# ScalarE and VectorE in program order, and seven products for gate and up in a feed-forward trunk

## The chip, the cores and the metric

The kernel runs on one core of a Trainium2 chip. The metric is the device time of one execution in microseconds (us). A core has TensorE (PE; its weight loads are listed as PEld), VectorE (DVE), ScalarE (ACT), GpSimd (POOL) and SyncE (SP), each with its own queue, and 16 DMA engines that they share.

## The reference

Two layers. Each layer adds half of a gated feed-forward to x, then two attentions of one input projection, then half of a second feed-forward. So there are four feed-forward stages, of this form:

```python
def rms_norm(x, g):
    y = x * rsqrt(mean(x * x, -1) + 1e-6)
    return y * g
def swiglu(h, w_gate, w_up, w_down):
    return (silu(h @ w_gate) * (h @ w_up)) @ w_down
x = x + 0.5 * swiglu(rms_norm(x, ffn_norm[l]), w_gate[l], w_up[l], w_down[l])
```

x is 256 tokens by 1024 features, the hidden width is 2816, everything is float32. A last RMSNorm gives the output.

## The kernel before

**Operands in two parts.** Every float32 operand of a large matmul is split into a high part, rounded to the float32r format, and the rest, also float32r. A product is then three matmuls: high by high, low by high, high by low (`tokens`, L323 to L332). The split of a weight tile is made in `emit_load` (L91 to L119): SP loads the raw tile (L100), ScalarE casts it to the high part (L116), VectorE subtracts (L117), in two halves of 128 x 1024 elements. Raw, high and low tiles have three buffers each (N_RAW, N_HI, N_LO). `specs` lists the weight tiles in the order of use; `weights()` (L122 to L129) gives the next one and has loads and splits written up to LOOK = 2 tiles ahead.

**A feed-forward stage** (`ffn`, L397) goes through the hidden width in groups of 512 columns: group 0, then groups 1 to 4 in a loop, then a last piece of 256 gate and 256 up columns. For a group, gate and up (256 tokens by 512 columns each) are 4 weight tiles of 512 features by 512 columns; each tile is 24 matmuls of 128x128 by 128x512 (4 chunks of features, 2 halves of the tokens, 3 matmuls). `hidden` takes them out of PSUM: ScalarE's SiLU (L402), VectorE's product (L408). `turn` transposes the hidden tile on TensorE (8 transposes, L70), and ScalarE and VectorE split it (L336, L337). `down` adds the group's part of the down product to four PSUM banks that stay for the whole stage (2 tiles, 48 matmuls). So a loop turn is 96 + 48 matmuls and 8 transposes. The other four PSUM banks go round.

**The norm** (`Norm`, L174) isn't applied ahead of the matmuls: x is transposed in four pairs of 128-feature blocks (`pair`), scaled by the gain and split (`operands`, L197 and L198); the row factor, from the sums of squares (L183) and a power on POOL (L208), is applied to the outputs. The residual sums (L382) of the second half and the last two pairs come inside the next stage's first group (`late`).

**What sets the order.** Matmuls and transposes outside a few attention parts are kept in program order (`mm`, `flip`). The instructions of the other engines are ordered by a scheduler at build time, from priorities and an estimated timeline; `urgent` raises the priority of what takes results out of PSUM. Each engine then runs its queue strictly in order.

Of the kernel before, what the change touches and what calls it, by code (L numbers as in the profile page):

```python
# [27 lines left out]
LOOK = 2  # L28
N_RAW, N_HI, N_LO = 3, 3, 3
N_S4 = 18  # L30
# [3 lines left out]
def trunk(ctx: ExitStack, tc: tile.TileContext, x, n1, g1, u1, d1, nm, w_in, sink,  # L34
          lq1, lk1, lq2, lk2, subln, w_out, n2, g2, u2, d2, nf, out):
    nc = tc.nc
    pe, act, dve, pool, sp = nc.tensor, nc.scalar, nc.vector, nc.gpsimd, nc.sync
# [27 lines left out]
    def mm(*a, **k):  # L65

        tc.keep_in_program_order(pe.matmul(*a, **k))  # L67

    def flip(*a):
        tc.keep_in_program_order(pe.transpose(*a))  # L70

# [4 lines left out]

    specs = []
    loaded = {}
# [7 lines left out]
    def plain(w, c0, n, k0=0, kn=None):  # L86
        src = rows(w, c0, n, k0, kn)
        kn = src.shape[1]
        return (kn, n, lambda t: [(t, src)])

    def emit_load(i):  # L91
        kn, n, moves = specs[i]
        raw = wp.tile([P, kn, n], F32, tag="raw", bufs=N_RAW, name=nm_("raw"))
# [4 lines left out]
        for dst, src in moves(raw):  # L98
            if i > 1:
                sp.dma_start(dst, src)  # L100
            else:
                for a, b in zip(cuts, cuts[1:]):
                    sp.dma_start(dst[:, a:b], src[:, a:b])  # L103
                    yield
# [15 lines left out]
    nxt = [0, 0]  # L120

    def weights():  # L122
        i = nxt[0]
        nxt[0] += 1
        while i > 1 and nxt[1] <= min(i + LOOK, len(specs) - 1):
            for _ in emit_load(nxt[1]):
                pass
            nxt[1] += 1
        return loaded.pop(i)  # L129

    for l in range(DEPTH):
        def ffn_specs(wg, wu, wd):
# [3 lines left out]
            for g in range(1, NGRP):  # L136
                specs.extend(plain(w[l], g * 512, 512, k0, 4) for w in (wg, wu) for k0 in (0, 4))
                specs.extend(down(g - 1, h) for h in range(2))
            for k0 in (0, 4):
                def gu_moves(t, k0=k0, ws=(wg[l], wu[l])):  # L140
                    return [(t[:, :, h * 256:h * 256 + 256], rows(w, FF - 256, 256, k0, 4)) for h, w in enumerate(ws)]
                specs.append((4, 512, gu_moves))
# [10 lines left out]
        for c in range(2):  # L153
            def qa_moves(t, c=c, wi=wi):
                return [(t[:, :, h * P:(h + 1) * P], rows(wi, QA + h * 256 + c * P, P)) for h in range(2)]
            paired.add(len(specs))
            specs.append((KC, 256, qa_moves))
# [5 lines left out]
        for k0 in (0, 2):  # L163
# [3 lines left out]
            specs.append((2, D, o_moves))  # L167
# [6 lines left out]
    class Norm:  # L174


        def __init__(self, g0):
            self.g0, self.xs = g0, []
            self.ss = tmp("nss", 2, (P, 2, 4))

        def squares(self, t, c, n):
            j_ = tmp("junk", 2, (P, 512))
            act.activation(j_[:, :n], xk[:, t, c:c + n], AF.Square, accum_out=self.ss[:, t, c // 256:c // 256 + 1])  # L183

        def pair(self, j):
            sl = halves(bank())
            for i in range(2):
                for t in range(2):
                    flip(sl[:, i, t * P:(t + 1) * P], xk[:, t, (2 * j + i) * P:(2 * j + i + 1) * P], ident)
            with urgent():  # L190
                self.operands(j, sl)

        def operands(self, j, sl):
            xs = blk()
            for i in range(2):
                g = gcol[:, self.g0 + 2 * j + i:self.g0 + 2 * j + i + 1]
                self.last_act = act.activation(xs[:, i, 0:S], sl[:, i], AF.Identity, scale=g)  # L197
                self.last = dve.scalar_tensor_tensor(xs[:, i, S:512], in0=sl[:, i], scalar=g, in1=f(xs[:, i, 0:S]),  # L198
                                                     op0=ALU.mult, op1=ALU.subtract)
            self.xs.append(xs)  # L200
# [11 lines left out]
        def spread(self, sl):  # L212
# [4 lines left out]
            mm(sl[:, 0:S], lhsT=ones, rhs=dg, start=True, stop=True)  # L217
# [7 lines left out]
    pool.dma_start(grow1, n1.rearrange("l (k p) -> (l k) p", p=P))  # L225
    early = [emit_load(0), emit_load(1)]
# [4 lines left out]
    nxt[1] = 2  # L231
# [13 lines left out]
    def take_x(k):  # L245

        if k < 4:
            norm.pair(k)
            for e in early * 2 if k < 2 else ():
                next(e)  # L250
        else:
            with tc.issue_after(norm.last_act.ins):
                for t in range(2):
                    for h in range(2):
                        norm.squares(t, h * 512, 512)
            norm.stats()

    grow = const.tile([NG - 16, P], F32, name="grow")
    dist_i = const.tile([P, 512], mybir.dt.int32, name="dist_i")
# [7 lines left out]
    lin = const.tile([P, 4, DEPTH * 64], F32, name="lin")  # L267
    lsum = const.tile([P, 2, DEPTH], F32, name="lsum")
    lpr = const.tile([P, 2, DEPTH * 64], F32, name="lpr")
# [5 lines left out]

    def attention_constants():
        for i, g in enumerate((nm, n2)):
            pool.dma_start(grow[i * 16:(i + 1) * 16], g.rearrange("l (k p) -> (l k) p", p=P))
        pool.dma_start(grow[32:34], subln)
# [3 lines left out]

        pool.iota(dist_i, pattern=[[P, 2], [-1, S]], base=0, channel_multiplier=1)
        dflat = distB.rearrange("p a b -> p (a b)")
        aflat = distA.rearrange("p a b -> p (a b)")
        dve.tensor_copy(aflat, dist_i)
# [3 lines left out]


        for c in range(4):
            pool.memset(qscA[0:64, c:c + 1], -0.125 / slopeA[c])
            pool.memset(qscA[64:128, c:c + 1], -0.125 / slopeA[c + 4])
            pool.memset(qscB[:, c:c + 1], -0.125 / slopeB[c])


        pool.dma_start(snk_in, sink.rearrange("l h -> (l h)").partition_broadcast(P))
        sv = snk_in.rearrange("p (l s c) -> p l c s", l=DEPTH, s=2)  # L300
        for t in range(2):
            for l in range(DEPTH):
                pool.tensor_copy(snk[:, l, :, t, :], sv[:, l])
        pool.tensor_scalar(nsnk.rearrange("p a b c d -> p (a b c d)"), snk.rearrange("p a b c d -> p (a b c d)"),
                           -1.0, 0.0, op0=ALU.mult, op1=ALU.add)

        for i, a in enumerate((lq1, lk1, lq2, lk2)):
            pool.dma_start(lin[:, i], a.rearrange("l d -> (l d)").partition_broadcast(P))

    def make_lam():  # L310
        for i in range(2):
            pool.tensor_tensor(lpr[:, i], lin[:, 2 * i], lin[:, 2 * i + 1], op=ALU.mult)
# [10 lines left out]
    def tokens(accs, xs, w, k0, ks=range(4), first=0, last=KC - 1, order=None):  # L323

        hi, lo = w
        for k, t in (order or [(k, t) for k in ks for t in range(2)]):
# [3 lines left out]
            mm(accs[t], lhsT=xh, rhs=hi[:, k], start=kk == first, stop=False)  # L330
            mm(accs[t], lhsT=xl, rhs=hi[:, k], start=False, stop=False)
            mm(accs[t], lhsT=xh, rhs=lo[:, k], start=False, stop=kk == (last if isinstance(last, int) else last[t]))  # L332
# [11 lines left out]
    def narrow(acc, w, j, xs, kcs, first, last):  # L344

        hi, lo = w
        for i, (wk, xk) in enumerate(kcs):
# [3 lines left out]
            mm(acc, lhsT=wh, rhs=xv[:, 0:S], start=first and i == 0 and j == 0, stop=False)  # L351
            mm(acc, lhsT=wh, rhs=xv[:, S:512], start=False, stop=False)
            mm(acc, lhsT=wl, rhs=xv[:, 0:S], start=False, stop=last and i == len(kcs) - 1 and j == 1)

    def first_groups(norm, ws):

        sls = [halves(bank()) for _ in ws]
        for k in range(0, KC, 2):
            if k:
                norm.late(k // 2 + 1)  # L360
# [12 lines left out]
    class Residual:  # L373
# [5 lines left out]
        def add(self, h, t):  # L379
            xv = xk[:, t, h * 512:(h + 1) * 512]  # L380
            with urgent():
                dve.tensor_tensor(xv, xv, self.accs[h][t], op=ALU.add)  # L382

        def turn(self, h):
            for j in (2 * h, 2 * h + 1):
                self.nxt.pair(j)
# [3 lines left out]
        def late(self, k):  # L390

            if k == 2:
                self.turn(1)
            elif k == 3:
# [431 lines left out]
```

## Time and profile before

| | |
|---|---|
| median of 3 runs | 979.01 us (977.41 to 979.86) |
| the profiled execution | 977.06 us, its span 975.3 us |
| granted TensorE clock, mean | 0.998 |
| ScalarE busy | 475.1 us (49%) |
| read from HBM | 167.54 MB, 173 GB/s over the span |
| a raw tile of 1024 KB, issue to landing | median 4.9 to 5.1 us |

The profile is one execution. A line of a group gives the source line, the engine, the operation, output and inputs with shapes and how often; behind the first bar the busy time and the mean of one in ns; behind the second the idle time of the engine just ahead, and what ended it. A line of the timeline gives start, duration and instruction. The chain of work follows what ended last back to the start. Busy PE is modelled: matmuls overlap, so the time from one start to the next counts, not the duration of one.

### The profile page before, as it was taken

The numbers are of one execution on the slowest core, as the hardware profiler recorded it, in microseconds if no ns is written. First come the engines' busy times: TensorE is split into PE (matmuls) and PEld (weight loads), VectorE is DVE, ScalarE is ACT, GpSimd is POOL, SyncE is SP. The second block draws the span as 40 slices with busy tenths as digits, with TensorE's granted clock in tenths as the row PEclk, the third lists the DMA queues.
The fourth block names the chain that finished last, engine by engine and source line by source line (L and its number), as shares of the span: only waits on it lengthen the run. The fifth ranks groups of instructions, "written<-read, shape, count | busy, mean of one in ns | idle before, by whom it ended". The sixth has DMA issues, their size and how long they took to land.

```text
span 975.3 us, 12345 instructions
## 1 busy us (share of the span) xinstructions
PE 954.0 (98%) x4940; PEld 808.2 (83%) x4940; DVE 555.4 (57%) x850; ACT 475.1 (49%) x779; POOL 22.0 (2%) x50
## 2 busy tenths in 40 slices
PE   7999999999999999999999999999999999999997
PEld 5788888899897888888888888888999878888886
DVE  4755455569955554454565454456797455554453
ACT  5643443458834543434464443436576454434433
POOL 4000000000000000000000000000000000000001
PEclk9999999999999999999999999999999999999999
DMA  9655565545523655555555555555553246565531
GB/s 275 228 199 173 180 208 173 185 149 179 137 87 130 215 173 183 200 179 194 193 174 175 191 196 176 200 184 173 174 148 112 87 173 197 191 202 202 179 130 43
DMA packets 98217, 169.38 MB, mean 174 GB/s; under 512 B 3182, under 2 KB 30896, under 8 KB 98160
## 3 DMA queue, kind: packets, MB, share of 16 engines
q1 hardware_dynamic: 96784, 167.26, 52.4%
q0 software_dynamic: 288, 0.30, 0.4%
q10 hardware_dynamic: 1088, 1.05, 0.3%
q8 instruction: 38, 0.62, 0.3%
q14 instruction: 19, 0.16, 0.0%
HBM read 167.54 MB, written 1.05 MB: 173 GB/s over the span
## 4 chain that ended last, share of the span: by engine, by line
PE 93%; DVE 3%; DMA 2%; issue 1%; ACT 0%; SPq 0%; POOLq 0%; POOL 0%
PE ps L67 85%; PE ps L70 3%; DMA raw<-in_ffn_w_gate_dram 2%; DVE wlo L117 2%; PE ps L547 1%; PE ps L612 1%; PE ps L633 1%; PE ps L635 1%; PE ps L634 1%; PE ps L652 1%; DVE s L198 1%; DVE xk L382 0%; ACT whi L116 0%; ACT s L197 0%; SPq L103 0%
## 5 line engine op out<-in xcount | busy, mean ns | idle before, releaser
L67 PE MATMUL ps<-whi,s 128*128 128x512 f32 (+1 forms) x2252 | 697.9, 391 | 7.4 <-DVE s L198 5.6
L117 DVE TENSOR_TENSOR wlo<-raw,whi 128x1024 fp32r<-128x1024 f32 (+2 forms) x392 | 379.5, 1014 | 322.6 <-ACT whi L116 320.5
L67 PEld LDWEIGHTS ps<-whi,s 128*128 128x128 f32 x2252 | 420.1, 188 | 96.4 <-DVE s L198 8.2
L116 ACT CAST whi<-raw 128x1024 fp32r<-128x1024 f32 (+2 forms) x392 | 323.8, 882 | 344.0 <-PE ps L67 299.1
L67 PE MATMUL ps<-wlo,s 128*128 128x512 f32 (+1 forms) x1126 | 437.8, 389 | 0.0
L67 PEld LDWEIGHTS ps<-wlo,s 128*128 128x128 f32 x1126 | 211.7, 188 | 43.5
L67 PE MATMUL ps<-s,whi 128*128 128x256 f32 x448 | 82.7, 286 | 0.4 <-DVE s L198 0.4
L67 PEld LDWEIGHTS ps<-s,whi 128*128 128x128 f32 x448 | 70.1, 192 | 1.6 <-DVE s L198 0.8
L67 PE MATMUL ps<-s,wlo 128*128 128x256 f32 x224 | 63.3, 283 | 0.0
L402 ACT ACTIVATE tmp<-ps,r 128x512 f32<-128x512 f32 (+1 forms) x48 | 31.2, 651 | 61.7 <-PE ps L67 61.7
L408 DVE SCALAR_TENSOR_TENSOR s<-ps,hr,tmp 128x512 f32<-128x512 f32 (+1 forms) x48 | 32.7, 705 | 36.9 <-PE ps L67 27.4
L67 PEld LDWEIGHTS ps<-s,wlo 128*128 128x128 f32 x224 | 42.9, 192 | 0.0
L557 ACT ACTIVATE s<-s,negm 128x256 f32<-128x256 f32 x64 | 31.8, 498 | 9.6 <-DVE negm L555 9.6
L337 DVE TENSOR_TENSOR s<-ps,s 128x512 fp32r<-128x512 f32 x48 | 31.0, 683 | 6.1 <-ACT s L336 6.1
L197 ACT ACTIVATE s<-ps,gcol 128x256 fp32r<-128x256 f32 x48 | 21.7, 472 | 21.9 <-PE ps L70 19.0
L336 ACT CAST s<-ps 128x512 fp32r<-128x512 f32 x48 | 25.8, 583 | 9.5 <-PE ps L70 9.5
L198 DVE SCALAR_TENSOR_TENSOR s<-ps,gcol,s 128x256 fp32r<-128x256 f32 x48 | 22.2, 480 | 11.0 <-ACT s L197 10.6
L70 PE MATMUL ps<-ident,s 128*128 128x128 f32 x208 | 27.3, 272 | 0.0
L70 PEld LDWEIGHTS ps<-ident,s 128*128 128x128 f32 x208 | 24.3, 141 | 3.3
L183 ACT ACTIVATE junk<-xk 128x512 f32<-128x512 f32 x24 | 15.0, 627 | 14.2 <-DVE xk L382 14.2
L208 POOL TENSOR_TENSOR r<-ms,mhalf 128x2 f32<-128x2 f32 x6 | 4.2, 705 | 628.1 <-DVE ms L206 628.1
L382 DVE TENSOR_TENSOR xk<-xk,ps 128x512 f32<-128x512 f32 x20 | 13.6, 681 | 3.8 <-PE ps L67 3.8
(109 smaller groups left out, 347.4 us busy)
## 6 DMA issues: line engine op xcount, KB each, us to landing
raw<-in_ffn_w_down_dram SPq DMA_DIRECT2D x44, 1024.0 KB, 4.9
raw<-in_ffn_w_gate_dram SPq DMA_DIRECT2D x39, 1024.0 KB, 5.0
raw<-in_ffn_w_up_dram SPq DMA_DIRECT2D x39, 1024.0 KB, 5.0
raw<-in_w_in_dram SPq DMA_DIRECT2D x14, 1024.0 KB, 5.1
raw<-in_ffn_w_gate_dram SPq DMA_DIRECT2D x8, 512.0 KB, 3.6
raw<-in_ffn_w_up_dram SPq DMA_DIRECT2D x8, 512.0 KB, 4.6
raw<-in_w_in_dram SPq DMA_DIRECT2D x8, 512.0 KB, 4.4
raw<-in_w_out_dram SPq DMA_DIRECT2D x4, 1024.0 KB, 4.7
```

Of the source, the lines that this page charges most:

```text
L67: tc.keep_in_program_order(pe.matmul(*a, **k))
L70: tc.keep_in_program_order(pe.transpose(*a))
L116: act.copy(h_, r_)
L117: dve.tensor_tensor(l_, r_, f(h_), op=ALU.subtract)
L183: act.activation(j_[:, :n], xk[:, t, c:c + n], AF.Square, accum_out=self.ss[:, t, c // 256:c // 256 + 1])
L197: self.last_act = act.activation(xs[:, i, 0:S], sl[:, i], AF.Identity, scale=g)
L198: self.last = dve.scalar_tensor_tensor(xs[:, i, S:512], in0=sl[:, i], scalar=g, in1=f(xs[:, i, 0:S]), op0=ALU.mult, op1=ALU.subtract)
L336: act.copy(dst[:, :, 0:S], src)
L337: dve.tensor_tensor(dst[:, :, S:512], src, f(dst[:, :, 0:S]), op=ALU.subtract)
L402: act.activation(g[:, :n], acc, AF.Silu, scale=norm.r[:, t:t + 1])
L408: dve.scalar_tensor_tensor(h[:, t, :n], in0=acc, scalar=norm.hr[:, t:t + 1], in1=g, op0=ALU.mult, op1=ALU.mult)
L557: act.activation(e[:, t, c], e[:, t, c], AF.Exp, scale=-1.0, bias=negm[:, n:n + 1], accum_out=den[:, n:n + 1])
```

## The change

**Program order.** ScalarE and VectorE, as TensorE, are wrapped so that each instruction outside attention is kept in program order. `urgent` and the other hints go.

**Seven products.** In groups 1, 3 and 4 of each stage (`SEVEN`), gate and up together are seen as a product of 2 by 2 blocks: token halves by feature halves, and feature halves by (gate, up). Strassen's scheme in Winograd's form does it in seven block products of 12 matmuls, in place of eight. `make_sums` forms the four sums of activation blocks once for each stage, each split into two parts; for them, `operands` keeps unsplit copies (`xg`), made on ScalarE. The sums of weight blocks are made in the raw tiles: with A, D the upper and lower gate blocks and B, C the upper and lower up blocks, step 0 uses A; step 1 B + C, where the C is added to the loaded B by a DMA from POOL's queue; step 2 A + B + C, by VectorE in the same tile; step 3 is a tile of the down matrix; step 4 D; step 5 A + B + C + D, by VectorE; step 6 A + B, where the B is added to the tile of A by a DMA, after step 2's sum; step 7 C; step 8 the second down tile. Each sum is split into high and low as any tile. `by_seven` runs the products in the order p1, p7, p6, down, p2, p4, p5, p3, down, and VectorE adds them up.

**Loads.** Raw tiles have six buffers, and loads run up to eight steps ahead of use (`AHEAD`); splits stay two ahead. Blocks of activations have 16 buffers in place of 18. POOL's constants are written at the start; what makes lambda moves from behind the first feed-forward into `attention_constants`, which is called ahead of group 3 of the first stage.

**Smaller moves.** SiLU is written right behind the gate's matmuls. In `ffn_close` and at the end of attention the next norm's first pairs are transposed earlier and among the last matmuls, and the residual sums of the first half after attention are made in quarters.

```diff
-LOOK = 2
-N_RAW, N_HI, N_LO = 3, 3, 3
-N_S4 = 18
+LOOK, AHEAD = 2, 8
+N_RAW, N_HI, N_LO = 6, 3, 3
+N_S4 = 16
+SEVEN = (1, 3, 4)
...
+            def call(*a, **k):
+                ins = issue(*a, **k)
+                if kept[0]:
+                    tc.keep_in_program_order(ins)
+                return ins
...
+    pe, act, dve = Kept(nc.tensor), Kept(nc.scalar), Kept(nc.vector)
...
+        def gather(k, to):
+            def add():
+                pool.dma_start(raws[to], w[k], accum_op=ALU.add)
+            return add
+        def plus(x, to):
+            def prep():
+                for h in (0, 2):
+                    x_, t_ = [raws[i][:, h:h + 2] for i in (x, to)]
+                    dve.tensor_tensor(t_, t_, x_, op=ALU.add)
+            return prep
...
+        return [Step(4, 512, load(a), key=a, free=[]),
+                Step(4, 512, load(b), key=b, behind=gather(c, b), free=[]),
+                Step(**n, prep=both(plus(a, b), gather(b, a)), src=b, free=[]),
+                downs[0],
+                Step(4, 512, load(d), key=d, free=[]),
+                Step(**n, prep=plus(b, d), src=d, free=[b, d]),
+                Step(**n, src=a),
+                Step(4, 512, load(c), key=c),
+                downs[1]]
...
+    def ahead(n):
+        n = min(n, len(specs) - 1)
+        while True:
+            if at["split"] <= n and at["prep"] > at["split"]:
+                for _ in emit_split(at["split"]):
+                    pass
+                at["split"] += 1
+            elif at["prep"] <= min(n + 1, len(specs) - 1) and at["dma"] > at["prep"] and \
+                    (specs[at["prep"]].prep is None or at["split"] >= at["prep"]):
+                if specs[at["prep"]].prep is not None:
+                    specs[at["prep"]].prep()
+                at["prep"] += 1
...
+        def make_sums(self):
+            (t0, t1), (b0, b1) = [(t[:, :, 0:P], t[:, :, P:S]) for t in self.xg]
+            self.sm = []
+            def make(x, y, op):
+                v = tmp().rearrange("p a (c s) -> p (a c) s", c=2)
+                dve.tensor_tensor(v, x, y, op=op)
+                sm = blk().rearrange("p a (c s) -> p (a c) s", c=2)
+                act.copy(sm[:, :, 0:P], v)
+                dve.tensor_tensor(sm[:, :, P:S], v, f(sm[:, :, 0:P]), op=ALU.subtract)
+                self.sm.append(sm)
+                return v
+            s1 = make(b1, t1, ALU.subtract)
+            s2 = make(s1, t0, ALU.add)
+            make(t1, t0, ALU.subtract)
+            make(b0, s2, ALU.subtract)
...
+        def prod(xo):
+            hi, lo = weights()
+            acc = bank()
+            for k in range(4):
+                xh, xl = xo(k)
+                pe.matmul(acc, lhsT=xh, rhs=hi[:, k], start=k == 0, stop=False)
+                pe.matmul(acc, lhsT=xl, rhs=hi[:, k], start=False, stop=False)
+                pe.matmul(acc, lhsT=xh, rhs=lo[:, k], start=False, stop=k == 3)
+            return acc
+        def by_seven(h, g):
...
+            p1 = prod(norm.quarter(0, 0))
+            m1 = flat()
+            act.copy(m1, p1)
+            p7 = prod(norm.summed(2))
+            hT = turn(h, 2)
+            p6 = prod(norm.summed(1))
+            u2 = put(flat(), p6, m1, ALU.subtract)
+            u3 = put(flat(), p7, u2, ALU.add)
+            down(hT, g - 1, 0, weights())
+            h = blk(F32)
+            p2 = prod(norm.quarter(0, 1))
+            g0 = put(m1, p2, m1, ALU.add)
+            silu(g0, g0, 0)
+            p4 = prod(norm.quarter(1, 1))
+            g1 = put(flat(), p4, u3, ALU.subtract)
+            silu(g1, g1, 1)
+            p5 = prod(norm.summed(0))
+            put(u3, u3, p5, ALU.subtract)
+            put(u2, u2, p5, ALU.subtract)
+            up(h, u3, g1, 1)
+            p3 = prod(norm.summed(3))
+            put(u2, u2, p3, ALU.add)
+            up(h, u2, g0, 0)
+            down(hT, g - 1, 1, weights())
+            return h
...
+        for n in range(1, NGRP):
+            if n == 3 and aside is not None:
+                aside()
+            if n in SEVEN:
+                h = by_seven(h, n)
+                continue
...
         before(2)
-        for sl in (gs, us):
-            tokens(sl, norm.xs, weights(), 4)
+        tokens(gs, norm.xs, weights(), 4)
+        g = gate(gs)
+        tokens(us, norm.xs, weights(), 4)
+        h = hidden(g, us)
```

363 lines of the change are left out of this document (218 added, 145 removed).

## The prediction

> **What bounds the kernel now.** I read part 1 of the page first, then the stretches of one steady group of a feed-forward stage, then that group's queues, then the groups by shape for prices.
>
> ```profile
> PE 954.0 (98%) x4940; PEld 808.2 (83%) x4940; DVE 555.4 (57%) x850; ACT 475.1 (49%) x779; POOL 22.0 (2%) x50
> ...
> 549.00:582.50 33.50, 33.50 (x154) 27.81 (x153) 16.79 (x16) 14.11 (x17) 0.00 (x0) 1.00 0.57 188
> ...
> 549.01 32.67 PE ps L67 x144
> 581.69 0.87 PE ps L70 x8
> 582.56 32.66 PE ps L67 x144
> ```
>
> The second line is the table of stretches (PE, PEld, DVE, ACT, POOL busy, granted clock, DMA share, GB/s), the last three are from the chain of work. TensorE has no hole in a group: 144 matmuls in 32.67 us, so 0.2269 us from one to the next, and 8 transposes in 0.87 us; a group lasts 33.55 us. VectorE is busy for half of it, 16.8 us. So TensorE sets the end now, and every matmul taken out is worth 0.227 us as long as nothing else is late.
>
> Prices and queues:
>
> ```profile
> L117 DVE TENSOR_TENSOR wlo<-raw,whi 128x1024 fp32r<-128x1024 f32 x256 | 302.3, 1222 | 282.4 <-ACT whi L116 280.5
> L116 ACT CAST whi<-raw 128x1024 fp32r<-128x1024 f32 x256 | 256.3, 1050 | 290.0 <-PE ps L67 274.0 <-issue 11.8 <-ACT whi L116 2.3
> L337 DVE TENSOR_TENSOR s<-ps,s 128x512 fp32r<-128x512 f32 x48 | 31.0, 683 | 6.1 <-ACT s L336 6.1
> L408 DVE SCALAR_TENSOR_TENSOR s<-ps,hr,tmp 128x512 f32<-128x512 f32 x40 | 28.8, 750 | 27.5 <-PE ps L67 27.4
> L402 ACT ACTIVATE tmp<-ps,r 128x512 f32<-128x512 f32 x40 | 27.4, 688 | 50.5 <-PE ps L67 50.5
> L382 DVE TENSOR_TENSOR xk<-xk,ps 128x512 f32<-128x512 f32 x20 | 13.6, 681 | 3.8 <-PE ps L67 3.8
> ...
> 566.26 2.36 DVE L117 TENSOR_TENSOR wlo<-raw,whi 128x1024 fp32r<-128x1024 f32 x2 [2.96 <-ACT whi L116]
> 570.16 1.43 DVE L408 SCALAR_TENSOR_TENSOR s<-ps,hr,tmp 128x512 f32<-128x512 f32 x2 [1.54 <-PE ps L67]
> ```
>
> One half of a weight split costs VectorE 1.222 us alone; two back to back take 2.36, so a half takes 1.14 us of a full queue. ScalarE's cast of a half is 1.05. The idle times say who waits for whom today: ScalarE's cast waits for TensorE to free a buffer, VectorE for the cast. Both have room.
>
> **The change, part by part.** (All times against the profiled execution: 977.06 us, span 975.3; the median shown is 979.01, 2 us above it.)
>
> *Matmuls out.* Gate and up of a group are eight products of 12 matmuls (96); now seven (84). Twelve groups (3 in each of 4 stages) save 144 matmuls: 144 x 0.2269 = **-32.7 us** if TensorE stays the bound. A seven-group then needs 132 x 0.2269 + 0.87 = 30.8 us of TensorE.
>
> *VectorE in a seven-group.* Splits: seven sums of weights and two of the down matrix, 18 halves x 1.14 = 20.6 us (12 halves before). Two weight sums stay on VectorE, 4 halves; no row adds two SBUF tensors in fp32, the nearest is L117 (same shape, same two sources), 1.14 each, 4.6 us. Seven sums of products from PSUM (nearest L382 and L337, 0.68 alone, 0.64 in a row): 4.5. Two L408: 1.4. Two L337: 1.3. Sum **32.4 us, more than TensorE's 30.8** (ScalarE's: 18 casts x 0.95 in a row and 4 to 5 us, 22). VectorE becomes the longer queue inside a run of seven-groups.
>
> *Program order.* VectorE and ScalarE now take their work strictly as written, so a handoff VectorE to ScalarE to VectorE is idle time on VectorE once it is the bound. In by_seven the casts of the next split stand behind silu(g0) on ScalarE, and silu(g0) behind VectorE's sum g0: after g0 VectorE waits 0.69 (L402) + 1.05 (cast) = 1.7 us, and again after g1: 3.5 us. The cast of step 2 stands behind VectorE's sum of that step: 1.05. So a seven-group that follows a seven-group takes 32.4 + 3.5 + 1.05 = **36.9 us**, longer than the 33.55 of before. Queued behind each of these waits are the next split (TensorE waits for it two steps later) and the later sums. What eases it: splits run two steps ahead (LOOK 2), a head start of 2 x 2.3 = 4.6 us, used up once in a run. Group 3 (after plain group 2): 36.9 - 4.6 = 32.3. Groups 3 and 4: 69.2 against 67.1 before. Group 1 follows the stage's head (next), which uses about half of the start: 34.6. Three groups: 103.8 against 100.65, **+3.1 a stage**.
>
> *Sums of the activations.* make_sums stands in program order behind the norm's statistics and ahead of the splits for the second half of `up`. From the stage's first matmul: 24 matmuls 5.45, transposes 0.87, then ScalarE does eight scalings (L197, 0.472) and two squares (0.63 + 0.19), to about 11.0; reduction, scale, POOL's power (0.70) and one more, to 12.3; four times sum 0.68, ScalarE copy 0.58, difference 0.68, each waiting for the last, 7.8: VectorE is free at 20.1. The cast of the fourth weight tile is behind the last copy: its first half is ready at 21.8. TensorE wants it at 11.8 + 5.45 = 17.2. **+4.6 a stage**. If VectorE had other work between, nothing; that is the lower end.
>
> *Four stages*: (3.1 + 4.6) x 4 = +31 us.
>
> *Loads and the two DMAs that add.* HBM traffic grows by 2 MB in each of 12 groups. Part 3's four shares make 53.4% at 174 GB/s, so all engines busy would move 326 GB/s; 1.05 MB takes 3.2 us of them, and a seven-group's six plain loads take 19 us and leave 18 of 37 for the two adds. No row shows an adding DMA. Lower bound: a plain load (4.9 us issue to landing, 3.2 of the engines). Upper: three passes (read, read, write), 9.6. I take two, 6.4, nearest to the plain load row, and hidden: the next group's sum has from the split of step 5 to the split of the next step 1, four splits, two handoffs and seven sums, 9.2 + 3.5 + 5 = 18 us, and needs 4.9 + 0.6 (POOL's issue row) + 6.4 + 1.7 = 13.6.
> The Trainium skill (DMA: Bandwidth & Descriptors, Measured) gives 6.15 us for a plain 1 MB transfer from GpSimd's queue; by it, doubled for the second read as an estimate of mine, the add would take 12.3 us and the late rival below would come true; no row here shows such a transfer.
>
> POOL's issues: four took 0.55 us each from 6.54 to 8.70, with L117 on VectorE from 6.79 to 8.08, and three 0.49 to 0.52 before, with VectorE idle. So VectorE doesn't hold them back. The Trainium skill (SBUF — State Buffer, Who interferes with whom) says that a VectorE instruction with two SBUF inputs blocks a GpSimd instruction that reads SBUF; by that rule each add could start one L117 (1.22 us) later, and the late rival would be likelier. The trace shows no such stretch.
>
> *Edges.* Where attention hands over, the trace shows matmuls waiting for operands because VectorE and ScalarE took a weight split first:
>
> ```profile
> 303.22 0.50 PE L67 MATMUL ps<-whi,s 128*128 128x512 f32 x1 [0.49 <-DVE s L198]
> ...
> 305.39 0.50 PE L67 MATMUL ps<-whi,s 128*128 128x512 f32 x1 [0.72 <-ACT s L197]
> 306.87 0.50 PE L67 MATMUL ps<-whi,s 128*128 128x512 f32 x1 [0.98 <-DVE s L198]
> ```
>
> The starts are 0.88, 1.12 and 1.48 us after the one before where 0.23 is normal: 2.8 us, in both layers. Program order puts operands ahead of splits, and six raw tiles bring the weights earlier: -5.6. The same kind of holes at 22 to 29 us add up to 3.9; I take half, -1.9, since the loads there are at 0.91 of the DMA engines. Against it: lambda's Exp moves into group 3 of the first stage, two table loads (1.283 each): +1.5 after cover. Attention itself and the tail I cost at nothing: their instructions stay. SP's queue too: it issues the same loads earlier, and POOL's queue, now with two waiting DMAs a group ahead of the norms' powers, has them hidden as long as the loads of b land in time.
>
> **Sum:** 977.1 - 32.7 is what a still-bound TensorE would give; but the groups don't reach it. Direct: 977.1 + 31 - 5.6 - 1.9 + 1.5 = 1002.1. Beside the median that is 1004; I put **1002**.
>
> **Rivals.**
> A (forecast): VectorE bounds the seven-groups through the handoffs, 1002. For: 32.4 against 30.8. Against: 57% busy on average, room on both sides. Its own range, from prices 5% either way (1.4 us a seven-group, 17 in all): 985 to 1020.
> B: VectorE keeps pace. Without handoffs groups 3 and 4 need 64.8 - 4.6 = 60.2, under TensorE's 61.6. Then -32.7 - 6 and only the heads cost 18.4: **957**; 939 if the heads are hidden too. Decides: that ScalarE has cast the next half before VectorE asks.
> C, slower too: an add takes over about 9 us. Then VectorE stands at the split of step 1 (it takes its work in order, so the product sums and TensorE behind it), some 2 us for each us over (two adds a group in a row on the same engines), where a group follows close: at 12 us +10 a stage, **1042**.
> D: half of the handoffs and half of the head are covered. Group 1: 32.3, groups 3 and 4: 64.6, the head +2.3: -1.4 a stage, -6 in all, and -6 at the edges: **965**.
> The side that ends otherwise than my forecast is B; that the seven products aren't built can't be, the matmul count shows it.
>
> **How the numbers follow.** A 0.46, B 0.19, C 0.17, D 0.18. Slower by over 0.3% (what a measurement here tells from no change): A and C, 0.63. Faster: B and 0.13 of D, 0.32; the rest of D, where less is covered, the same (0.04) or slower (0.01). Range 952 to 1035: it leaves out B's far end (0.07) and C beyond 1035 (0.1).
>
> **What would show it.** Matmul rows: 144 fewer of 128x512. In group 4 of a stage TensorE's holes released by "DVE wlo" and VectorE's idle time released by "ACT whi" right after the two silu, 1.7 us each; group 4 at about 37 us, group 3 at 32. A hole of some 4.6 us in the middle of each stage's first group. If the groups run at 30.8 without holes, A is wrong and B right. If VectorE or ScalarE waits for a DMA on raw, it is C; the landing times of POOL's DMAs would tell their length.

## The result, and the profile after

The kernel after takes 1028.34 us (median of 4 runs, 1027.0 to 1028.53), beside 979.43 us for the kernel before on the same chip (4 runs, 977.41 to 981.99): a ratio of 1.050, 95% interval 1.048 to 1.052. The direction is the forecast one; the loss, 49 us, is twice the forecast one, 23. The time lies beyond the range that I gave for rival A, the forecast, by itself (985 to 1020). The profiled execution's span is 1025.2 us, 49.9 us above that of before.

Part 1 of the page of the kernel after, its row of clock by slices, its chain of work by engine, and the two costliest groups of VectorE and ScalarE:

```profile
PE 950.1 (93%) x4796; PEld 784.4 (77%) x4796; DVE 763.6 (74%) x1090; ACT 576.3 (56%) x913; POOL 51.8 (5%) x73
...
PEclk9899999999999899999998999999999999999999
...
PE 58%; DVE 25%; ACT 10%; issue 4%; DMA 2%; POOL 1%; SPq 1%; ACTq 0%; POOLq 0%; DVEq 0%
...
L50 DVE TENSOR_TENSOR wlo<-raw,whi 128x1024 fp32r<-128x1024 f32 (+2 forms) x464 | 461.0, 1046 | 129.0 <-ACT whi L50 127.0
...
L50 ACT CAST whi<-raw 128x1024 fp32r<-128x1024 f32 (+2 forms) x464 | 393.6, 908 | 174.5 <-PE ps L50 87.8
```

The chain and VectorE's splits before:

```profile
PE 93%; DVE 3%; DMA 2%; issue 1%; ACT 0%; SPq 0%; POOLq 0%; POOL 0%
...
L117 DVE TENSOR_TENSOR wlo<-raw,whi 128x1024 fp32r<-128x1024 f32 (+2 forms) x392 | 379.5, 1014 | 322.6 <-ACT whi L116 320.5
```

4796 TensorE rows in place of 4940: the 144 matmuls are gone. But the chain is TensorE's for only 58% (93% before), and 35% of it is VectorE's and ScalarE's. VectorE, which is now on the path, still stood idle for 127 us waiting for casts (320.5 before, when that cost next to nothing). Three slices show a lower clock (8). The holes of before at 303 to 307 us, where attention hands over, have no counterpart: the second stage's first 73 matmuls and transposes follow each other without one.

Every wrapped instruction has the helper's line (L50), so I read by tile, and by the time from one group's first 512-wide matmul to the next one's, in us:

| stage | group 0 | 1 | 2 | 3 | 4 | last piece |
|---|---|---|---|---|---|---|
| before, 2nd stage | 25.74 | 34.34 | 33.54 | 33.54 | 33.54 | 10.99 |
| after, 2nd stage | 32.38 | 34.29 | 33.53 | 32.06 | 35.93 | 11.79 |
| before, 3rd stage | 22.70 | 34.33 | 33.55 | 33.53 | 33.54 | 10.98 |
| after, 3rd stage | 35.20 | 32.18 | 33.53 | 32.07 | 36.02 | 11.79 |

(Eight transposes changed sides between group 1 and the last piece: 0.8.) Groups 3 and 4 came out as forecast, 32.3 and 36.9. The loss is in group 0, the head: +6.0, +6.6, +12.5 and +6.7 in the four stages. And the two stretches from a first feed-forward's last matmuls into attention, nowhere in the forecast, grew by 4.3 each.

**Group 4** follows the forecast's mechanism. VectorE in the third stage's group 4:

```profile
672.86 0.69 DVE L50 TENSOR_TENSOR tmp<-ps,tmp 128x512 f32<-128x512 f32 x1
675.27 2.36 DVE L50 TENSOR_TENSOR wlo<-raw,whi 128x1024 fp32r<-128x1024 f32 x2 [1.73 <-ACT whi L50]
677.55 0.69 DVE L50 TENSOR_TENSOR tmp<-ps,tmp 128x512 f32<-128x512 f32 x1
679.96 2.36 DVE L50 TENSOR_TENSOR wlo<-raw,whi 128x1024 fp32r<-128x1024 f32 x2 [1.73 <-ACT whi L50]
```

The same 35.9 us as a stretch (length; then PE, PEld, DVE, ACT and POOL busy, granted clock, DMA share, GB/s):

```profile
653.10:689.00 35.90, 32.18 (x141) 25.24 (x140) 32.18 (x34) 22.37 (x25) 1.28 (x1) 1.00 0.73 216
```

After g0 and after g1 (0.69 each) VectorE waits 1.73 us: silu, then the cast. Its busy time in the group is 32.18 us, forecast 32.4.

**The head.** ScalarE in the second stage's head, from the late pairs' scalings to the weight casts behind the sums:

```profile
326.86 0.47 ACT L50 ACTIVATE s<-ps,gcol 128x256 fp32r<-128x256 f32 x1
328.83 0.48 ACT L50 ACTIVATE s<-ps,gcol 128x256 fp32r<-128x256 f32 x1 [1.50 <-DVE s L50]
329.86 1.21 ACT L50 ACTIVATE s<-ps,gcol 128x256 f32<-128x256 f32 x3 [0.55 <-DVE s L50]
331.61 0.47 ACT L50 ACTIVATE s<-ps,gcol 128x256 fp32r<-128x256 f32 x1 [0.55 <-DVE s L50]
332.64 0.84 ACT L50 ACTIVATE s<-ps,gcol 128x256 f32<-128x256 f32 x2 [0.55 <-DVE s L50]
...
340.89 0.62 ACT L50 CAST s<-tmp 128x512 fp32r<-128x512 f32 x1 [1.36 <-DVE tmp L50]
342.87 0.62 ACT L50 CAST s<-tmp 128x512 fp32r<-128x512 f32 x1 [1.36 <-DVE tmp L50]
343.40 3.88 ACT L50 CAST whi<-raw 128x1024 fp32r<-128x1024 f32 x4
```

Read the brackets: in each pair, the second scaling and the unsplit copies behind it wait for VectorE's difference of the scaling before, and each copy of a sum waits until VectorE has made that sum, behind the difference of the one before. The first wait is the longest, 1.50 us, because VectorE still had a weight split ahead of the pair's first difference:

```profile
326.04 2.36 DVE L50 TENSOR_TENSOR wlo<-raw,whi 128x1024 fp32r<-128x1024 f32 x2 [2.02 <-ACT whi L50]
328.32 0.48 DVE L50 SCALAR_TENSOR_TENSOR s<-ps,gcol,s 128x256 fp32r<-128x256 f32 x1
```

Four weight casts stand behind all that, at 343.40. TensorE, in the second stage's head and twice in the third's:

```profile
344.49 1.22 PE L50 MATMUL ps<-whi,s 128*128 128x512 f32 x2 [7.41 <-ACT whi L50]
...
522.40 1.22 PE L50 MATMUL ps<-whi,s 128*128 128x512 f32 x2 [2.14 <-ACT whi L50]
...
544.32 1.22 PE L50 MATMUL ps<-whi,s 128*128 128x512 f32 x2 [5.36 <-ACT whi L50]
```

And the table of stretches around the first of these (the granted clock is the third number from the right):

```profile
319.70:335.10 15.40, 15.40 (x73) 12.80 (x72) 6.90 (x13) 10.44 (x24) 0.00 (x0) 1.00 0.48 155
335.10:342.80 7.70, 1.98 (x9) 1.31 (x7) 4.74 (x9) 1.85 (x3) 0.72 (x1) 0.91 0.00 0
342.80:348.50 5.70, 3.97 (x9) 2.72 (x10) 4.76 (x6) 5.61 (x6) 0.00 (x0) 0.52 0.13 14
```

After the hole the granted clock is 0.52: the first starts are 0.59 to 0.67 us apart, the next four 0.427, and soon 0.227 again. Summed over these starts that is 2.1 us more than at 0.227; 1.9 and 2.8 after the third stage's two holes.

### The profile page after: what moved, and what is told of

Same layout as the page of the kernel before. It is cut to its first block, busy times and chain, and to the rows that moved or that the text cites. A ratio compares the mean times of both kernels' runs of the same rounds, so it can differ in the third digit from the quotient of the medians.

```text
span 1025.2 us, 12592 instructions
## 1 busy us (share of the span) xinstructions
PE 950.1 (93%) x4796; PEld 784.4 (77%) x4796; DVE 763.6 (74%) x1090; ACT 576.3 (56%) x913; POOL 51.8 (5%) x73
## 3 DMA queue, kind: packets, MB, share of 16 engines
q0 software_dynamic: 12928, 25.46, 14.5%
## 4 chain that ended last, share of the span: by engine, by line
PE 58%; DVE 25%; ACT 10%; issue 4%; DMA 2%; POOL 1%; SPq 1%; ACTq 0%; POOLq 0%; DVEq 0%
PE ps L50 58%; DVE wlo L50 15%; ACT whi L50 5%; DVE s L50 4%; ACT s L50 3%; DVE tmp L50 3%; DVE raw L50 3%; DMA raw<-in_ffn_w_up_dram 1%; ACT junk L50 1%; ACT tmp L50 1%; DMA xk<-in_x_dram 1%; SPq L159 1%; DVE xk L50 0%; ACT L50 0%; POOL r L345 0%
## 5 line engine op out<-in xcount | busy, mean ns | idle before, releaser
L50 PE MATMUL ps<-whi,s 128*128 128x512 f32 (+1 forms) x2220 | 701.0, 396 | 48.7 <-ACT whi L50 37.8
L50 DVE TENSOR_TENSOR wlo<-raw,whi 128x1024 fp32r<-128x1024 f32 (+2 forms) x464 | 461.0, 1046 | 129.0 <-ACT whi L50 127.0
L50 PEld LDWEIGHTS ps<-whi,s 128*128 128x128 f32 x2220 | 416.9, 190 | 144.5 <-ACT whi L50 46.9
L50 ACT CAST whi<-raw 128x1024 fp32r<-128x1024 f32 (+2 forms) x464 | 393.6, 908 | 174.5 <-PE ps L50 87.8
L50 PE MATMUL ps<-wlo,s 128*128 128x512 f32 (+1 forms) x1110 | 438.5, 395 | 10.1 <-DVE wlo L50 9.9
L50 PEld LDWEIGHTS ps<-wlo,s 128*128 128x128 f32 x1110 | 210.6, 190 | 67.1 <-DVE wlo L50 24.4
L50 PE MATMUL ps<-s,whi 128*128 128x256 f32 x448 | 83.0, 286 | 1.4 <-ACT whi L50 1.4
L50 PEld LDWEIGHTS ps<-s,whi 128*128 128x128 f32 x448 | 70.0, 191 | 2.8 <-ACT whi L50 1.8
L50 ACT ACTIVATE s<-ps,gcol 128x256 fp32r<-128x256 f32 (+1 forms) x80 | 35.1, 472 | 58.6 <-PE ps L50 30.9
L50 PE MATMUL ps<-s,wlo 128*128 128x256 f32 x224 | 63.5, 284 | 1.5 <-DVE wlo L50 1.5
L127 POOL DMA_DIRECT2D raw<-in_ffn_w_up_dram x24 | 31.2, 1300 | 576.4 <-DVE wlo L50 186.8
L50 DVE TENSOR_TENSOR raw<-raw,raw 128x1024 f32<-128x1024 f32 x48 | 56.5, 1221 | 0.0
L50 ACT CAST s<-ps 128x512 fp32r<-128x512 f32 x48 | 26.0, 589 | 53.2 <-PE ps L50 53.2
L50 ACT ACTIVATE tmp<-tmp,r 128x512 f32<-128x512 f32 x24 | 17.4, 724 | 62.8 <-DVE tmp L50 62.8
L50 DVE SCALAR_TENSOR_TENSOR s<-ps,gcol,s 128x256 fp32r<-128x256 f32 x48 | 22.8, 482 | 34.6 <-ACT s L50 34.6
L50 DVE TENSOR_TENSOR s<-ps,s 128x512 fp32r<-128x512 f32 x48 | 31.1, 686 | 18.1 <-ACT s L50 18.1
L50 PEld LDWEIGHTS ps<-s,wlo 128*128 128x128 f32 x224 | 42.9, 191 | 1.9 <-DVE wlo L50 1.9
L50 PE MATMUL ps<-ident,s 128*128 128x128 f32 x304 | 41.0, 277 | 1.8 <-DVE s L50 1.8
L50 PEld LDWEIGHTS ps<-ident,s 128*128 128x128 f32 x304 | 35.8, 143 | 7.0 <-DVE s L50 2.4
L50 ACT ACTIVATE s<-s,negm 128x256 f32<-128x256 f32 x64 | 31.8, 499 | 7.4 <-DVE negm L50 7.4
L50 DVE TENSOR_TENSOR tmp<-ps,tmp 128x512 f32<-128x512 f32 x48 | 33.0, 687 | 0.4
L50 ACT CAST s<-tmp 128x512 fp32r<-128x512 f32 (+1 forms) x22 | 13.1, 599 | 28.0 <-DVE tmp L50 28.0
```

Source lines behind the costliest of these rows:

```text
L50: ins = issue(*a, **k)
L127: pool.dma_start(raws[to], w[k], accum_op=ALU.add)
```

## The experiments

All are edits of the kernel after, timed against the kernel before on the chip that ran them (its medians there: 979.8 to 981.1 us). The question: is it program order as such, the amount of work, the place of the sums, or the handoffs?

### Without the seven products

```diff
-SEVEN = (1, 3, 4)
+SEVEN = ()
```

> SEVEN is empty: no seven products, no sums of weights or activations, no unsplit copies; program order, deeper loads and the smaller moves stay. Theory O (program order itself costs time, at the places where ScalarE's and VectorE's scalings of the next stage stand ahead of the weight splits): the four edges stay longer than before, +4.3 at each feed-forward to attention edge and +3 at the first hole of the second layer's first stage, the start gains 2; groups are 33.5 again; 983 to 990 us, slower than before by 0.5 to 1%. Theory S (all the loss belongs to the seven products and their sums; program order gains what the forecast had it gain, 5.6 at the hand-overs and 1.9 at the start): 968 to 973, faster than before.

977.91 us, ratio 0.998 (0.997 to 1.000): between the two. Both theories hold in part and cancel: the start is 1.9 us earlier and the second and fourth head 3.1 shorter (22.67 in place of 25.74; forecast 2.8 each), but the two stretches into attention are 4.3 longer. So the 50 us come with the seven products and their sums, in this order of the queues. Against this kernel, the heads of the kernel after cost +7.1, +9.7, +12.0 and +9.8, together **38.6**; group 1 +6.4 in the first stage and 0.1 in the rest together; group 3 -4.0 and group 4 +9.7 over all stages.

### The sums written later

```diff
             norm.stats()
-            if norm.sums:
-                norm.make_sums()
...
-        tokens(gs, norm.xs, weights(), 4)
+        w = weights()
+        if norm.sums:
+            norm.make_sums()
+        tokens(gs, norm.xs, w, 4)
```

> make_sums is written one step later in each stage: behind the splits of the third and fourth next tiles, in place of ahead of them. Theory P (the place of the sums is the cost: TensorE stands 5.4 to 8 us in the middle of every first group because two weight splits are queued behind the sums, and its clock is lowered for some us after that): the first groups fall from 32.4 to 35.2 us by 6 to 8 each, and at most 2 of it comes back where the second product of group 1 needs the sums; 995 to 1005. Theory W (VectorE's and ScalarE's work in the head is too much in whatever order): the hole moves into group 1, which grows by what the first group loses; 1020 to 1030.

1031.4 us, ratio 1.052 (1.050 to 1.054), 1.4 above the range of theory W. My theory P is out: the heads of stages 2 and 4 fall to 23.0, and their group 1 grows to 44.5. ScalarE shows why moving alone does nothing:

```profile
349.15 0.62 ACT L50 CAST s<-tmp 128x512 fp32r<-128x512 f32 x1 [1.36 <-DVE tmp L50]
349.78 1.28 ACT L50 ACT_TABLE_LOAD   x1
351.08 1.27 ACT L50 ACTIVATE tmp<-ps,r 128x512 f32<-128x512 f32 x2
352.23 1.99 ACT L50 CAST whi<-raw 128x1024 fp32r<-128x1024 f32 x2
```

The chain of sums now has SiLU and its table load behind it, and behind these the cast that TensorE wants at about 347. The hole is 6.3 us (from start to start, less 0.227), one tile later.

### The hand-overs

```diff
             act.activation(xs[:, i, 0:S], sl[:, i], AF.Identity, scale=g)
+        for i in range(2):
+            g = gcol[:, self.g0 + 2 * j + i:self.g0 + 2 * j + i + 1]
             dve.scalar_tensor_tensor(xs[:, i, S:512], in0=sl[:, i], scalar=g, in1=f(xs[:, i, 0:S]),
...
+        ahead(at["use"] + LOOK - 1)
         for j in range(2):
             nxt.pair(j)
         res.squares(0)
         group(1, [(2, t) for t in range(2)])
-        ahead(at["use"] + LOOK - 1)
```

> Two edits at the hand-overs: both scalings of a pair are written ahead of both differences, and in ffn_close the next stage's first two splits are written ahead of the next norm's pairs and squares. Theory O: the holes at the two feed-forward to attention edges (some 4.3 each) and the first hole of the second layer's first stage (2.3, with the slow matmuls behind it some 4) go, the sums stay where they are; 1016 to 1021. Rival W (the work of ScalarE and VectorE at the edge is too much in any order): what the splits gain the pairs lose; 1026 to 1031.

1014.54 us, ratio 1.035 (1.033 to 1.037): 14 us less, more than theory O asked. The stretches into attention give 3.0 each, the third stage's head 5.3 (its first hole is gone), the other heads up to 1.1, and the fourth stage's group 1 another 1.1; the third stage's group 1 loses 0.8. The two edits were not run apart.

### The splits ahead of silu

```diff
             g0 = put(m1, p2, m1, ALU.add)
+            w = weights()
             silu(g0, g0, 0)
-            p4 = prod(norm.quarter(1, 1))
+            p4 = prod(norm.quarter(1, 1), w)
```
(the same for g1 and p5)

> In by_seven the next tile's split is written ahead of silu(g0) and of silu(g1), so that the casts no longer stand behind an instruction that waits for VectorE. Theory A (the forecast's: the two waits of VectorE, 1.73 us each, are what makes group 4 36 us and not 32.5): group 4 falls by 3 to 3.5, group 3 by up to 1, the last piece by 0.8, some 19 in all; 1006 to 1012. Rival N (VectorE's queue is full of work and something else is late next, so the idle time moves to another place, or TensorE waits for SiLU's outputs in place of splits): less than 6 us; 1022 to 1029.

1008.60 us, ratio 1.029 (1.027 to 1.031): 20 us less, the sum of theory A, but not from its terms. Group 3 is 30.8 us in three stages and 31.4 in the first, TensorE's own time (the forecast's 30.8), 6.4 less over all stages where up to 4 was expected. Group 1 falls by 10.1 over all stages, which the theory didn't have. Group 4 stays at 33.8 to 36.0 and gives only 4.2 of the expected 12 to 14. So the waits at silu were a real cost, but that the total came out is in part luck. What is late next in group 4 is new:

```profile
630.45 1.99 ACT L50 CAST whi<-raw 128x1024 fp32r<-128x1024 f32 x2
640.95 2.00 ACT L50 CAST whi<-raw 128x1024 fp32r<-128x1024 f32 x2 [8.51 <-DMA raw<-in_ffn_w_up_dram]
```

ScalarE waits 8.5 us for an adding transfer, issued at 626.14 and landed at 640.6. Over the whole run such waits cost ScalarE 32.7 us; in the kernel after, 5.5. So the forecast's rival C stood right behind its rival A.

### The head without its sums

```diff
-            return lambda k: (self.sm[i][:, k, 0:P], self.sm[i][:, k, P:S])
+            return self.quarter(i % 2, i // 2)
```
(and make_sums isn't called)

> make_sums is left out: the four products that need sums of activation blocks take plain blocks instead, so gate and up come out as something else; the unsplit copies, the sums of weights and everything else stay. Theory Z (the four sums are the cost of the head, 7.3 us of VectorE and ScalarE in turns, wherever they stand): the first groups fall to about 24 to 28 us, and the slow matmuls behind the hole go with it; 990 to 1000. Rival X (the head is late because of the eight unsplit copies on ScalarE and because group 1 starts with its splits already late): first groups and groups 1 stay near their sizes; 1012 to 1022.

1001.90 us, ratio 1.022 (1.020 to 1.024), 26 us less, 1.9 above the range of theory Z. Heads 2 and 4 are 23.0, 0.3 above those of e1_noseven; the sums with their handoffs and the slow matmuls behind the hole are 6.3, 9.4, 7.7 and 9.4 us of the heads, 33 of the 38.6. The third stage's first hole stays (head 27.5), and the first stage's group 1 grows by 6. There ScalarE waits for an adding transfer, issued at 30.90 among the loads of the start and landed 13.5 us later:

```profile
44.43 1.99 ACT L50 CAST whi<-raw 128x1024 fp32r<-128x1024 f32 x2 [6.51 <-DMA raw<-in_ffn_w_up_dram]
```

### The sums regrouped in place

```diff
-                dve.tensor_tensor(sm[:, :, P:S], v, f(sm[:, :, 0:P]), op=ALU.subtract)
...
+            for v, sm in zip(vs, self.sm):
+                dve.tensor_tensor(sm[:, :, P:S], v, f(sm[:, :, 0:P]), op=ALU.subtract)
```

> make_sums stays where it is, but its operations are regrouped: the four sums on VectorE, with ScalarE's four copies beside them, and then the four differences, in place of four times sum, copy, difference. Theory L (half of what the sums cost is waiting in turns, 4 x 0.68 us of VectorE a stage, and each us of the hole costs some more in slow matmuls): the hole in the middle of the first groups falls by 2.7 to 3; 1013 to 1018. Rival W (VectorE and ScalarE have other work queued that is late next): 1023 to 1029.

1015.50 us, ratio 1.036 (1.034 to 1.038): 13 us less, theory L. The second and fourth head fall by 3.1 and 3.2: VectorE's four waits add up to 2.7, and the stretch at the low clock is shorter (3.4 us in place of 6.8).

### All mends together

The edits at the hand-overs, at silu and of the regrouping, the sums at the later place, and the next split written ahead of group 0's SiLU:

```diff
         tokens(gs, norm.xs, w, 4)
+        w = weights()
         g = gate(gs)
-        tokens(us, norm.xs, weights(), 4)
+        tokens(us, norm.xs, w, 4)
```

> Together: the pairs' scalings ahead of their differences and the splits ahead of the pairs (as in e3_pairs), splits ahead of both silu in by_seven (as in e4_silu), the sums regrouped and written behind the splits of the third and fourth next tiles, and the split of the fifth ahead of group 0's SiLU. Theory of separate terms: 14 + 20 + about 12 for the regrouping off 1028, 980 to 985. If order is all that the sums lacked, the hole in front of group 1's second product falls from 6.3 to about 2.5 as well: 965 to 978, faster than before. Rival C (the adding transfers land too late once VectorE is quicker): group 1 and group 4 stay at 34 to 36 us; 985 to 1000.

977.73 us, ratio 0.998 (0.997 to 0.999): 0.2% below the kernel before, just inside the range for "order is all" (965 to 978). Heads 2 to 4 are 22.7. But group 1 is 33.9 to 34.8 (43.4 in the first stage, where an adding transfer lands late again) and group 4 34.1 to 38.0, as rival C had it. The second stage's group 1 in the table of stretches, and ScalarE at the start of the third stage's group 4:

```profile
335.20:369.90 34.70, 31.73 (x141) 25.36 (x140) 34.63 (x39) 25.19 (x30) 1.32 (x1) 1.00 0.69 211
```
```profile
621.79 2.00 ACT L50 CAST whi<-raw 128x1024 fp32r<-128x1024 f32 x2 [8.07 <-DMA raw<-in_ffn_w_up_dram]
```

VectorE is busy 34.63 of 34.70 us: behind the head it is now simply full. In group 4 it is rival C again. These are two limits: VectorE's queue behind the head, and the late add where a seven-group follows a seven-group.

### The price of the adding transfer

```diff
-                pool.dma_start(raws[to], w[k], accum_op=ALU.add)
+                pool.dma_start(raws[to], w[k])
```
(on top of the splits ahead of silu; the kernel leaves out the two sums of weights that these transfers make)

> e4_silu with the two adding transfers of a group replaced by plain ones from the same queue to the same tiles, so that the sums of weights come out as something else (C for B + C, B for A + B). In e4_silu ScalarE stands 8.5 us and VectorE 4.5 us ahead of group 4 for such a transfer, which lands 14.8 us after its issue among four plain loads. Theory C (it is the second read of an adding transfer that makes it late): group 4 falls by 2 to 3.5 us a stage; 994 to 1002. Rival R (six raw tiles come free in a bunch, the loads that follow share the DMA engines with the add, and a plain transfer would be as late): group 4 stays within 1 us; 1004 to 1009.

993.36 us, ratio 1.013 (1.011 to 1.015): 15 us less than with the adds; group 4 is 30.81 to 30.86 in the last three stages. That is theory C, 0.6 below its range. The issue table, with the adds and without, us from issue to landing last:

```profile
raw<-in_ffn_w_up_dram POOLq DMA_DIRECT2D x24, 1024.0 KB, 9.0
```
```profile
raw<-in_ffn_w_up_dram POOLq DMA_DIRECT2D x24, 1024.0 KB, 5.9
```

Adding costs 3.1 us of landing; no run tells what of it is the second read.

### Seven products in groups 2 and 4

```diff
-SEVEN = (1, 3, 4)
+SEVEN = (2, 4)
```
(on top of all mends)

> e7_all_moved with seven products in groups 2 and 4 alone, so that each of them follows a plain group, where VectorE has about half of its time free. Theory V (VectorE is the bound in a run of seven-groups and in one that follows the head; it can carry any single one out of the spare time of a plain group): groups 1 and 3 take 33.5, groups 2 and 4 take 30.8 as group 3 did in e4_silu, the heads 22.7; against e7_all_moved 5.4 us less in each of the last three stages and about 15 in the first: 945 to 953, faster than before by 2.7 to 3.5%. Rival C (the adding transfers are late wherever they stand): groups 2 and 4 stay near 34 to 35; 962 to 972.

954.39 us, ratio 0.974 (0.972 to 0.976). Groups 2 and 4 are 30.8 in every stage (31.1 once): theory V; in the second stage VectorE is busy for 24.3 us of group 1's 33.7 and 28.8 of group 2's 30.8. It missed its range by 1.4 us, the first stage's group 1 being still 40.4.

### ScalarE and VectorE back to the scheduler

```diff
-    pe, act, dve = Kept(nc.tensor), Kept(nc.scalar), Kept(nc.vector)
+    pe, act, dve = Kept(nc.tensor), nc.scalar, nc.vector
```

> The kernel after with TensorE alone kept in program order; ScalarE and VectorE are ordered by the scheduler again, as in the kernel before, with the seven products, the sums and everything else as they are. Theory O (strict program order is what turns the new work into holes): the scheduler fills the waits between the sums and the pairs; 985 to 1005. Rival W (the work is too much, or the scheduler's own estimates order it no better): 1015 to 1035.

979.09 us (10 runs, 973.56 to 985.07), ratio 0.999 (0.996 to 1.002): 49 us less than in program order, with the same work. Theory O, and more than it asked: neither the seven products nor strict order costs the 50 us alone (e1_noseven has strict order), the two together do. VectorE in the second stage's head (L317 and L320 are the sums and their differences, L186 the weight splits, L134 a sum of weights):

```profile
332.46 0.68 DVE L317 TENSOR_TENSOR tmp<-s 128x512 f32<-128x512 f32 x1
333.06 1.22 DVE L186 TENSOR_TENSOR wlo<-raw,whi 128x1024 fp32r<-128x1024 f32 x1
334.20 0.68 DVE L317 TENSOR_TENSOR tmp<-s,tmp 128x512 f32<-128x512 f32 x1
334.80 1.22 DVE L186 TENSOR_TENSOR wlo<-raw,whi 128x1024 fp32r<-128x1024 f32 x1
335.94 0.69 DVE L320 TENSOR_TENSOR s<-tmp,s 128x512 fp32r<-128x512 f32 x1
336.54 1.22 DVE L134 TENSOR_TENSOR raw<-raw,raw 128x1024 f32<-128x1024 f32 x1
```

No line has a bracket: between the sums, where VectorE stands idle in strict order, it makes a split or a sum of weights. The last three heads are 22.7 to 22.9, group 4 of these stages 32.1 to 32.2.

### The base that they have to beat

Without seven products, with both edits at the hand-overs.

> e1_noseven with the two edits of e3_pairs (no seven products at all; program order with the pairs' scalings ahead of their differences, and the next splits ahead of the pairs). It prices program order and the deeper loads when the hand-overs are mended, and is the base that seven products have to beat. Theory O: the two feed-forward to attention edges give back 3 each; 969 to 973, faster than before by 0.7 to 1%. Rival W (without the unsplit copies the edges have no hole of that kind): 976 to 980, as e1_noseven.

971.11 us, ratio 0.991 (0.989 to 0.993). Theory O: 3.0 back at each stretch into attention.

### The sums in group 1

```diff
             g = gate(gs)
+            if n == 1 and norm.sums:
+                norm.make_sums()
             us = [bank(), bank()]
```
(groups 2 and 4, all mends; one sum's difference is written between the others)

> e9_two_four with the four sums made inside group 1, behind its SiLU (one sum's difference written between the others), where nothing needs them for another group; so no split of the head stands behind them. In e9_two_four group 1 of the first stage still takes 40.4 us, with one hole of 3.5 in front of its transposes and slow matmuls behind it; the other three groups 1 take 33.5 to 33.7. Theory V (VectorE's queue in the head is what makes that hole, the sums in it being 5.2 of its us): it falls to 33.6 to 35; 947 to 950. Rival D (the first stage is late because the DMA engines are full until 40 us, and the splits wait for data): it stays at 39 to 41; 953 to 956.

948.25 us (5 runs, 948.11 to 950.43), ratio **0.968** (0.967 to 0.970), the quickest. The first stage's group 1 is 33.54: theory V, the sums in the head's queue. The chain:

```profile
PE 97%; DMA 2%; DVE 0%; issue 0%; ACT 0%; POOLq 0%; POOL 0%; ACTq 0%
```

TensorE is the bound again. 96 matmuls fewer than in the base are 21.8 us at 0.2269; the two kernels differ by 22.9.

## Why the prediction failed, step by step

**Matmuls out**: right, -0.227 us each, but only where TensorE is the bound; the last kernel shows the gain, the kernel after lost it.

**VectorE in a seven-group, and program order within it**: right. 32.18 us busy against 32.4, two waits of 1.73 against 1.7, groups 3 and 4 at 68.0 against 69.2. Against e1_noseven the groups cost +12.2 us in all, forecast +12.4, though that is luck in part: 6.4 of it is the first stage's group 1, which begins behind the head's hole with slow matmuls and two shorter holes, and group 4 came out 1 us shorter than forecast.

**Sums of the activations, +4.6 a stage: the step that failed.** The heads cost 38.6, not 18.4. For the second stage: TensorE stopped 17.2 us after its first matmul (as forecast), and the chain of sums took 8.0 us (7.8). But the late pairs' eight scalings and two squares took 8.0 us, from 326.86 to 334.85, where I had added up busy times to 4.7. ScalarE stood idle for 3.15 us of it: the same turns of ScalarE and VectorE that I had counted in the sums I left out of the pairs, and a weight split that VectorE took first. And I had put the two squares at the price of one (0.8); they took 1.5. The pairs began 0.9 late too; 1.4 came back behind the last copy, where I had put too much. That makes the hole 7.6 us (from start to start, less 0.227), 3.0 more. Then the matmuls behind the hole cost another 2.1, a term that I didn't have. 7.6 + 2.1 = 9.7, as measured against e1_noseven. In the third stage there is another hole (at 522; 2.3 and 1.9 at the low clock), where pairs and squares are written ahead of the first splits; it is gone in e3_pairs.

**Edges**: the hand-over from attention gave 6.1 in two layers (forecast 5.6), the start 2.2 (1.9). That the other edges cost nothing was wrong, the second step that failed: +8.5 on the way into attention, from pairs and squares ahead of splits. It isn't the unsplit copies, since e1_noseven has none and the same loss; e3_pairs took back 6.0, the rest stays open. Of the 25 us by which the profiled run is above the sum of 1002.1, the heads are 20.2 and these edges 8.5; smaller gains take some back. What the move of lambda cost was not run by itself.

**Loads and adds**: nearly hidden in the kernel after, as forecast, with two passes of the engines: queue 0 took 14.5% of 1025.2 us; less the 3.9 us of its small loads (as before) that is 6.0 for each of 24 adds (forecast 6.4), where a plain load takes 3.1. They land after 9.7 us (median; 12.4 to 13.8 ahead of group 4), past the 9 that I named as the point from which rival C decides, and C came true as soon as group 4 got quicker. The Trainium skill (DMA: Bandwidth & Descriptors, Measured) has 6.15 us for a plain transfer of this size from this queue, without the making of its descriptors; the plain one here took 5.9 from the start of its issue. Doubling it to 12.3 was too much: adding cost 3.1 and not 6.15. That VectorE doesn't hold POOL's issues back is borne out as far as the length of an issue shows it: of the 24 issues of adds, the two that met no VectorE instruction (at 312.52 and 813.68) took 1.33 us, and the others, beside VectorE's work, 1.27 to 1.39. The later start that I drew from the Trainium skill (SBUF — State Buffer, Who interferes with whom) didn't follow from it: the rule is on GpSimd instructions that read SBUF, and no row here shows that an issue does.

**Rivals.** A's mechanism was right; its sum came short of the heads. B's condition, that ScalarE has cast before VectorE asks, comes nearest where the scheduler orders the queues; that gave 979 and not 957, with 32.1 to 32.4 us left in groups 3 and 4 of the last three stages and 41.5 in the first stage's group 1. D had the heads half covered; in strict order they cost twice what I put.

## What to carry to other kernels

In a strict order an exchange between two engines is idle time for both, unless other work is written between: in a chain, count latencies and not busy times, in old work as in new, and look at what is queued behind its end. A scheme that trades TensorE's work for VectorE's paid here where VectorE had room just before; spread such pieces out in place of putting them side by side, and put one-off work into the slackest group. When one wait is mended, look at the transfer that it hid.

## What the runs showed of the hardware

TensorE's clock fell behind short holes. In the kernel after, behind a gap of 2.5 us from one matmul's start to the next's (at 522.40), the matmuls started up to 0.67 and then 0.427 us apart, and 0.23 again within 3.5 us; behind gaps of 5.7 and 7.8 us the slow stretch was 5.3 and 3.9 us. Such a hole cost 1.9 to 2.8 us more than its length, and the longest did not cost the most. Length alone doesn't decide: a gap of 2.6 us in e5_nosums (at 15.53) left the granted clock at 1.0. The Trainium skill (TensorE: Matmul & The Clock Gate, What's actually happening) has the clock at half after an idle window of some 3.4 us, free-running, and back after as long a busy one. The trace agrees with the half rate (0.427 against 0.227) and with the windows (the granted clock of the kernel after is at half for 3.41 or 6.83 us at a time, until the last stretch, which the end cuts off); but the idle time needn't fill a window: a gap of 2.5 us was enough at 522.40.

An adding DMA of 1 MB takes the 16 engines twice as long as a plain load (6.0 against 3.1 us) and lands 3.1 us later than a plain one of the same queue (9.0 against 5.9); its issue keeps POOL busy for 1.30 us, where a plain one in e8_silu_plain takes 0.76 and I had put 0.6.
